# Layer 0's routing with one shared product moved up, and one expert's job in four f32 passes

## The chip, the cores and the metric

The kernel runs on one core of a Trainium2 chip. The metric is device time in microseconds: three runs gave 1667.2, 1667.28 and 1667.38 us, a median of 1667.28 us. The engines are TensorE (PE; PEld is its loading of weights), VectorE (DVE), ScalarE (ACT), GpSimd (POOL) and SyncE (SP), which here issues the loads of weights.

## The reference, cut to what matters

Two layers, each a mixer and then a mixture of experts with one shared expert. In layer 0 the mixture works on 512 tokens: 256 latent ones and 256 of context, four tiles of 128. The part that the change touches:

```python
def moe_ffn(h, w_router, e_bias, w_gate, w_up, w_down, s_gate, s_up, s_down):
    scores = sigmoid(h @ w_router)                     # 64 experts
    _, idx = top_k(scores + e_bias, 8)
    wts = take_along_axis(scores, idx); wts = wts / wts.sum(-1) * 2.5
    # each expert: its tokens, gathered
    a = silu(xb @ w_gate[e]) * (xb @ w_up[e])          # 1024 -> 256, twice
    yb = a @ w_down[e]                                 # 256 -> 1024
    routed = sum over experts of yb * weight
    shared = (silu(h @ s_gate) * (h @ s_up)) @ s_down
    return routed + shared
```

All of it is f32.

## The kernel before

Each layer has a plan, a list of jobs written out in `Plan`. A job is one block of up to 128 tokens. It holds one expert (a single), two of 64 rows (a pair), or parts of experts in lanes of 32 rows. Layer 0 has 42 jobs, numbered 0 to 41. Job 38 is a pair, job 39 is the single of the expert of rank 10, jobs 40 and 41 are pairs.

**The loop of jobs.** TensorE and SyncE run in the order in which the code is written (`manual_schedule`); the order on the other engines comes from the framework's scheduler. For job j the code issues the loads of its weights (`experts`, L1069 and L1074 on SyncE), computes gate and up (`gate_up`, L1337), applies the activation (`act`: ACT L1292, DVE L1293), adds fetched partial sums (`add_fetched`, DVE L1533), transposes job j + 1's tokens (`slots_T`, L1459), scatters pieces of job j - 1's output by a product with a matrix of ones and zeros (`scatter`, PE L1544, summed by DVE L1536), transposes the activation (`act_T`, L1308), computes down (`down`, L1351) and splits the output into two parts for its scatter (`place`, L161). The loads go into a ring of eleven buffers of 1 MB (`w8`). SyncE issues a load as soon as its buffer is free, and so runs ahead of TensorE.

**Four passes or three.** `passes[j]` chooses for a job. With 4 the operands are f32, and each product is one call. With 3 the tokens, the weights and the activation are split into a high and a low part in fp32r (`split`: ACT casts the high part, DVE subtracts it), and each product is three calls: high by high (L165), low by high (L166), high by low (L167). Gate and up are then split in four parts of 128 by 1024 (`gate_up3`), down in two (`down3`). In layer 0 every single after job 2 has 3: jobs 6, 11, 15, 20, 25, 29, 34 and 39.

**The routing of layer 0** stands ahead of the loop, in the code's order. `sh_step(t)` advances the shared expert of tile t by one step: gate; up with the activation's start; transposing the activation (L1308); down with its copies to `acc` (L1351, DVE L1400). `route_step(t)` advances the routing of tile t: transposing `hp`, the normalized tokens (L1053); the router's product with the top 8 (L1130 to L1144). `route_T(t)` transposes the tile's router weights `sg` (L1150). `rank` counts the tokens of each expert (L1170 to L1188) and sorts the experts by count; its result `ordi` names the experts whose weights SyncE loads. `slots` marks which token stands where (DVE L1250 writes `oh`, PE L1258 and L1276 multiply by it, DVE L1280 follows).

Of the kernel before, what the change touches and what calls it, by code (L numbers as in the profile page):

```python
# [118 lines left out]
def tile_block(ctx: ExitStack, tc: tile.TileContext, I, out):  # L119
# [940 lines left out]
    def moe(l, out_of, nt, mp, pre=lambda: None, post=lambda: None):  # L1060
# [16 lines left out]
        def expert_dn(c, e):  # L1077
            d = I["moe_w_down"][l, e]
            if l == 0 or c % 4 != 1:
                return load_dn(d)  # L1080
            wd = [k4([128, D], "dn"), mp.tile([128, D], F32, name="dnx")]
            for j in range(2):
                S.dma_start(wd[j], d.rearrange("o (p j) n -> j p (o n)", j=2)[j])
            return wd
# [63 lines left out]
        def route_T(t):  # L1148
            p = bank()
            T.transpose(p[:NE, :128], sgs.pop(t), ident)  # L1150
            A.copy(wT[:, t], p[:NE, :128])
# [65 lines left out]
        njob = len(jobs)  # L1217
# [190 lines left out]
        def both(xs, j0, xT):  # L1408
            for k in range(2):
                xs[j0 + k] = lambda j, sl, k=k: xT[j // 4][:, j % 4, k * 128 + sl.start:k * 128 + sl.stop]  # L1410
# [33 lines left out]
        def gather(x, idx_col):  # L1444
            G.indirect_dma_start(out=x, out_offset=None, in_=h2d[:n2, :],  # L1445
                                 in_offset=bass.IndirectOffsetOnAxis(ap=idx_col, axis=0),
                                 bounds_check=n2 - 1, oob_is_err=False)

        def slots_T(x, passes):
            if passes == 3:  # L1450
                xT = [k4([128, NJ, 128], "xT", F32R) for _ in range(2)]
            else:
                xT = k4([128, NJ, 128], "xT")
            parts = [lambda j, sl, x=x: x[:, j, sl] for x in (xT if passes == 3 else [xT])]
            yield parts if passes == 3 else parts[0]
            for q in range(2):
                p = bank()
                for j in range(4):
                    T.transpose(p[:, j * 128:j * 128 + 128], x[:, (q * 4 + j) * 128:(q * 4 + j) * 128 + 128], ident)  # L1459
                src = p.rearrange("p (j s) -> p j s", j=4)  # L1460
                if passes == 3:
                    split(xT[0][:, q * 4:q * 4 + 4], xT[1][:, q * 4:q * 4 + 4], src)
                else:
                    A.copy(xT[:, q * 4:q * 4 + 4], src)
                yield

        def gather_mm(j0):

            two = range(j0, min(j0 + 2, njob))
            oh = k2([128, nt, 2, 128], "ohr", F32R)  # L1470
            for t in range(nt):
                for j in two:
                    for c, lane, m, off in jobs[j]:
                        V.tensor_scalar(oh[:, t, j - j0, 32 * lane:32 * (lane + m)], ib[:, off:off + 32 * m],
                                        pos[:, t, c:c + 1], None, op0=OP.is_equal)
            xT = [k4([128, 4, 256], "xT") for _ in range(2)]
            n = len(two) * 128
            yield xT
            for q in range(4):
                p = bank()  # L1480
                for j in range(2):
                    o = p[:, j * 256:j * 256 + n]
                    for t in range(nt):
                        for k in range(2):
                            T.matmul(o, h2p[t][k][:, 2 * q + j], oh[:, t].rearrange("p a b -> p (a b)")[:, :n],  # L1485
                                     start=t == 0 and k == 0, stop=t == nt - 1 and k == 1)
                A.copy(xT[q // 2][:, q % 2 * 2:q % 2 * 2 + 2, :n],
                       p.rearrange("p (j s) -> p j s", j=2)[:, :, :n])
                if q == 1:
                    yield  # L1490
# [184 lines left out]

        passes = []
        for sg_ in jobs:
            passes.append(3 if l == 0 and len(sg_) == 1 and len(passes) > 2 else 4)
        grp, sc = [], iter(())
        over = overflow()  # L1680
        LA = 3 if l == 0 else 2
        with tc.manual_schedule(engines={mybir.EngineType.SP, mybir.EngineType.PE}):
# [11 lines left out]
            def route_step(t):  # L1694
                if t not in routes:
                    routes[t] = route(t, hps.pop(t))
                next(routes[t])
# [22 lines left out]
            def sh_step(*ts):  # L1720
                for t in ts:
                    next(shs[t], None)
# [5 lines left out]
            def slots_until(j):  # L1728
                while ready[0] < min(j, njob):
                    next(more)  # L1730

            xs = {}
            if l == 0:
                sh_step(0, 0)
                route_T(0)
                route_T(1)
                route_step(2)
                sh_step(1, 0)
                route_step(2)
                sh_step(1)  # L1740
                route_step(3)
                sh_step(0)
                route_step(3)
                sh_step(1, 2, 2)
                route_T(2)
                next(rank)
                sh_step(1, 2)
                slots_until(n0)
                affine()
                for j in range(2):  # L1750
                    gather(xgs[j], idx[:, j:j + 1])
                next(rank)
                sh_step(3, 3)
                next(rank)
                sh_step(2)
                tr = slots_T(xgs[0], passes[0])
                xs[0] = next(tr)
                for _ in tr:
                    pass
                next(rank)  # L1760
                sh_step(3)
            else:
                sh_step(0, 0)
                route_step(1)
                sh_step(0)
                route_step(1)
                route_T(0)
                sh_step(0)
                next(rank)
                sh_step(1)  # L1770
                slots_until(n0)
                gm = gather_mm(0)
                affine()
                both(xs, 0, next(gm))
                next(gm)
                next(rank)
                for _ in gm:
                    pass
                next(rank)
                for c in range(NS, NS + 2):  # L1780
                    early[c] = expert_dn(c, ds(S.value_load(ordi[0:1, c:c + 1], min_val=0, max_val=NE - 1), 1))
# [153 lines left out]
    with tc.tile_pool(name="moe0", bufs=1) as mp:  # L1935
        normalize(moe(0, out0, 4, mp, preload_na, mods_na)[0], xt[:2])
# [3 lines left out]
    with tc.tile_pool(name="moe1", bufs=1) as mp:  # L1940
        y = moe(1, out1, 2, mp)[1]
        for t in range(2):
            for n in range(1 + t):
                r = slice(n * 512, n * 512 + D // (1 + t))
                S.dma_start(out[0, t * 128:t * 128 + 128, r], y[t][:, r])
# [85 lines left out]
```

## Time and profile before

| what | value |
|---|---|
| median of three runs | 1667.28 us |
| profiled execution, its own time | 1667.79 us |
| its span | 1666.0 us |
| PE busy | 1560.8 us, 94% |
| DVE busy | 762.9 us, 46% |
| ACT busy | 444.3 us, 27% |
| mean granted TensorE clock | 0.98 of full |
| layer 0's routing | about 240 to 296 us |
| layer 0's jobs | about 296 to 922 us |
| of these job 39 | 862.9 to 887.7 us |

A row of the timeline gives the start, the duration, the engine with line and operation, output and input, and in brackets how long the engine had been idle and what released it. Matmuls are pipelined, so durations overlap and the distance between starts is what one costs; one f32 matmul shows as two records. PEclk is the granted clock of TensorE: 1.00 is 2.4 GHz, 0.50 is 1.2 GHz.

### The profile page before, as it was taken

To read this page: it belongs to the slowest core of one execution; us is meant where nothing else is said; L and a number is where in the kernel's file an instruction comes from. 1 tells how busy PE (TensorE), PEld (TensorE's weight loads), DVE (VectorE), ACT (ScalarE), POOL (GpSimd) and SP (SyncE) were. 2 spreads that over 40 slices of the span, in tenths; PEclk is the share of its full clock that TensorE was granted. 3 is DMA by queue.
4 is the path that set the end of the run, shared out by engine and by line. 5 is a ranking of instruction groups with operands and counts; after the bars stand their busy time and mean duration, and the time that the engine had idled before them with its cause. 6 is when DMAs were issued, how large, how long until landed. Compare 5 with 4: busy or idle time off the path is not lost. (4 is left out here: it accounts for less than half of the span.)

```text
span 1666.0 us, 30733 instructions
## 1 busy us (share of the span) xinstructions
PE 1560.8 (94%) x12138; PEld 1005.9 (60%) x12138; DVE 762.9 (46%) x2077; ACT 444.3 (27%) x882; POOL 174.0 (10%) x162
## 2 busy tenths in 40 slices
PE   7999999999999999999998799999999988989995
PEld 5765687546556566565665577866756654546542
DVE  2475585425455445354566832347443422223225
ACT  2447311113132232232222243332222211112111
POOL 1003210123221121221110000011000000000000
PEclk9999999999999999999999899999999999999998
DMA  9947864799999999989998566247779999999994
GB/s 331 340 172 290 297 233 162 268 366 382 346 398 345 402 401 389 392 327 406 404 407 309 205 212 222 89 181 309 303 316 420 419 419 419 419 420 419 419 420 179
DMA packets 122819, 547.91 MB, mean 329 GB/s; under 512 B 12917, under 2 KB 21509, under 8 KB 74672
## 3 DMA queue, kind: packets, MB, share of 16 engines
q1 hardware_dynamic: 108032, 501.76, 75.6%
q0 software_dynamic: 14640, 44.15, 8.6%
q8 instruction: 97, 1.59, 0.4%
q14 instruction: 50, 0.41, 0.1%
HBM read 532.10 MB, written 21.58 MB: 332 GB/s over the span
## 5 line engine op out<-in xcount | busy, mean ns | idle before, releaser
L1337 PE MATMUL bank<-w,xT 128*32 128x256 f32 (+1 forms) x5696 | 462.8, 388 | 25.8 <-DMA w<-in_moe_w_up_dram 20.2
L1337 PEld LDWEIGHTS bank<-w,xT 128*32 128x32 f32 (+1 forms) x5696 | 276.5, 122 | 204.9 <-DMA w<-in_moe_w_up_dram 28.2
L1351 PE MATMUL bank<-w,aT 128*32 128x512 f32 (+2 forms) x1248 | 235.3, 599 | 3.0 <-ACT aT L1312 2.9
L1293 DVE SCALAR_TENSOR_TENSOR a<-s,wsl,bank 128x256 f32<-128x256 f32 x70 | 33.6, 480 | 407.4 <-ACT s L1292 407.4
L1292 ACT ACTIVATE s<-bank 128x256 f32<-128x256 f32 x70 | 26.9, 385 | 544.5 <-PE bank L1337 496.7
L1544 PE MATMUL bank<-yy,ss 128*128 128x512 f32 x560 | 159.0, 411 | 1.4 <-DVE yy L161 1.1
L1536 DVE TENSOR_TENSOR acc<-acc,bank 128x512 f32<-128x512 f32 x212 | 138.0, 683 | 43.3 <-PE bank L1544 41.6
L1351 PEld LDWEIGHTS bank<-w,aT 128*32 128x32 f32 (+2 forms) x1248 | 68.5, 123 | 120.0 <-issue 104.0
L1544 PEld LDWEIGHTS bank<-yy,ss 128*128 128x128 f32 x560 | 97.3, 191 | 25.9 <-DVE yy L161 5.0
L161 DVE TENSOR_TENSOR yy<-bank,yy 128x512 fp32r<-128x512 f32 x96 | 65.9, 689 | 91.7 <-ACT yy L161 91.7
L161 ACT CAST yy<-bank 128x512 fp32r<-128x512 f32 x96 | 56.2, 586 | 161.6 <-PE bank L1351 144.2
L1445 POOL DMA_INDIRECT xg<-h2d,idx x42 | 52.1, 1239 | 356.8 <-PE bank L1459 181.7
L161 DVE TENSOR_TENSOR wl<-half,wh 128x1024 fp32r<-128x1024 f32 x35 | 42.7, 1224 | 74.4 <-ACT wh L161 74.4
L1250 DVE TENSOR_SCALAR oh<-ib,pos 128x64 bf16<-128x64 bf16 (+3 forms) x432 | 68.7, 245 | 9.7 <-PE bank L1276 9.7
L1516 POOL DMA_INDIRECT accd<-yd,idx x37 | 59.4, 1605 | 128.0 <-issue 92.7
L165 PE MATMUL bank<-wh,hT 128*128 128x512 f32 x160 | 65.2, 407 | 1.7 <-ACT wh L161 1.1
L167 PE MATMUL bank<-wl,hT 128*128 128x512 f32 x160 | 63.4, 396 | 0.5 <-DVE wl L161 0.5
L166 PE MATMUL bank<-wh,hT 128*128 128x512 f32 x160 | 63.2, 395 | 0.3 <-DVE hT L161 0.2
L1485 PE MATMUL bank<-ohr,h2p 128*128 128x256 f32 x448 | 60.8, 289 | 0.0
L1485 PEld LDWEIGHTS bank<-ohr,h2p 128*128 128x128 f32 x448 | 55.3, 191 | 8.2 <-PE bank L1337 4.4
L1437 POOL TENSOR_TENSOR xr<-xr,tmp 128x512 f32<-128x512 f32 x2 | 3.3, 1649 | 478.2 <-DVE tmp L1436 478.2
L1459 PE MATMUL bank<-head,xg 128*128 128x128 f32 x336 | 52.1, 278 | 0.0
(362 smaller groups left out, 2313.2 us busy)
## 6 DMA issues: line engine op xcount, KB each, us to landing
w<-in_moe_w_gate_dram SPq DMA_DIRECT2D x128, 1024.0 KB
w<-in_moe_w_up_dram SPq DMA_DIRECT2D x128, 1024.0 KB
w<-in_moe_w_down_dram SPq DMA_DIRECT2D x104, 1024.0 KB
w<-in_w_mod_dram SPq DMA_DIRECT2D x24, 1024.0 KB
half<-in_na_w_in_dram SPq DMA_DIRECT2D x12, 1024.0 KB
mh<-in_w_mod_dram SPq DMA_DIRECT2D x12, 1024.0 KB
w<-in_w_mod_dram SPq DMA_DIRECT2D x16, 512.0 KB
row<-rowsd POOLq DMA_DIRECT2D x15, 512.0 KB, 8.3
```

Source lines behind the costliest of these rows:

```text
L161: return A.copy(o_h, src), eng.tensor_sub(o_l, src, o_h.bitcast(F32))
L165: T.matmul(p, xh, wh, start=first, stop=False)
L166: T.matmul(p, xl, wh, start=False, stop=False)
L167: T.matmul(p, xh, wl, start=False, stop=last)
L1250: V.tensor_scalar(oh[:, 32 * lane:32 * (lane + m)], ib[:, off:off + 32 * m], pos[:, t, c:c + 1], None, op0=OP.is_equal)
L1337: T.matmul(p[sl, q * FF:q * FF + FF], xT(j, sl), ws[k][0][q][:, j], start=j == 0, stop=j == NJ - 1, **kw)
L1351: T.matmul(p[sl], aT[:, j, sl], d[:, n * 512:n * 512 + 512], start=j == 0, stop=j == 1, **kw)
L1445: G.indirect_dma_start(out=x, out_offset=None, in_=h2d[:n2, :], in_offset=bass.IndirectOffsetOnAxis(ap=idx_col, axis=0), bounds_check=n2 - ...
L1485: T.matmul(o, h2p[t][k][:, 2 * q + j], oh[:, t].rearrange("p a b -> p (a b)")[:, :n], start=t == 0 and k == 0, stop=t == nt - 1 and k == 1)
L1516: G.indirect_dma_start(out=accd[turn_[0]][:, :], out_offset=bass.IndirectOffsetOnAxis(ap=i_, axis=0), in_=y[32 * lane:32 * (lane + m)], in ...
L1536: add = {0: lambda t, r, p: V.tensor_add(acc[t][:, r], acc[t][:, r], p)}
L1544: T.matmul(p, ss[:, t * 128:t * 128 + 128], yy[:, q, r], start=k == 0 and q == 0, stop=k == len(grp) - 1 and q == 1)
```

## The change

Two edits. First, `passes` gives 4 instead of 3 to a single from job 39 on (`njob - 3` is 39), so job 39 alone changes. Second, the first `sh_step` call of layer 0 also takes tile 1's gate product, ahead of `route_T(0)`, and a later call drops its step for tile 1, so that each of tile 1's steps comes one call earlier.

```diff
@@ -1675,7 +1675,7 @@
         passes = []
         for sg_ in jobs:
-            passes.append(3 if l == 0 and len(sg_) == 1 and len(passes) > 2 else 4)
+            passes.append(3 if l == 0 and len(sg_) == 1 and 2 < len(passes) < njob - 3 else 4)
@@ -1731,7 +1731,7 @@
             if l == 0:
-                sh_step(0, 0)
+                sh_step(0, 0, 1)
                 route_T(0)
                 route_T(1)
                 route_step(2)
@@ -1744,7 +1744,7 @@
                 sh_step(1, 2, 2)
                 route_T(2)
                 next(rank)
-                sh_step(1, 2)
+                sh_step(2)
```

On TensorE, from the end of tile 0's shared gate and up to tile 2's shared products, before (w_1828 is the shared gate, w_1830 up, w_1832 down):

```order
L1150 MATMUL bank<-head,sg 64x128 x2
L1053 MATMUL bank<-head,hp 128x128 x8
L1389 MATMUL bank<-w_1828,h2T 128x256 x8
L1308 MATMUL bank<-head,a 128x128 x2
L1130 MATMUL bank<-rw,h2T 128x64 x8
L1389 MATMUL bank<-w_1830,h2T 128x256 x8
L1053 MATMUL bank<-head,hp 128x128 x8
L1351 MATMUL bank<-w_1832,aT 128x512 x4
L1130 MATMUL bank<-rw,h2T 128x64 x8
L1308 MATMUL bank<-head,a 128x128 x2
L1389 MATMUL bank<-w_1828,h2T 128x256 x8
L1389 MATMUL bank<-w_1830,h2T 128x256 x8
```

The same place of TensorE now:

```order
L1389 MATMUL bank<-w_1828,h2T 128x256 x8
L1150 MATMUL bank<-head,sg 64x128 x2
L1053 MATMUL bank<-head,hp 128x128 x8
L1389 MATMUL bank<-w_1830,h2T 128x256 x8
L1308 MATMUL bank<-head,a 128x128 x2
L1130 MATMUL bank<-rw,h2T 128x64 x8
L1308 MATMUL bank<-head,a 128x128 x2
L1053 MATMUL bank<-head,hp 128x128 x8
L1351 MATMUL bank<-w_1832,aT 128x512 x4
L1130 MATMUL bank<-rw,h2T 128x64 x8
L1351 MATMUL bank<-w_1832,aT 128x512 x4
L1389 MATMUL bank<-w_1828,h2T 128x256 x8
```

Tile 1's gate product has moved ahead of the two transpositions of router weights, its up product ahead of tile 0's activation, and its down product (the second L1351) ahead of tile 2's gate; before, that down product stood behind the count of tokens.

On VectorE, at the marks of the first two jobs, in the code's `slots`:

```order
 L1250 TENSOR_SCALAR oh<-ib,pos 128x96
-L1400 COPY acc_2505<-bank 128x512
-L1250 TENSOR_SCALAR oh<-ib,pos 128x32
-L1250 TENSOR_SCALAR oh<-ib,pos 128x64 x6
-L1400 COPY acc_2505<-bank 128x512
-L1250 TENSOR_SCALAR oh<-ib,pos 128x64 x2
+L1250 TENSOR_SCALAR oh<-ib,pos 128x32
+L1250 TENSOR_SCALAR oh<-ib,pos 128x64 x8
 L1250 TENSOR_SCALAR oh<-ib,pos 128x32 x3
 L1280 TENSOR_TENSOR sm<-bank,jm 128x30
```

The two copies of tile 1's shared output no longer stand among the marks; they come earlier, in the routing of tile 3.

On TensorE, job 39 now (w_8772, w_8774 and w_8776 are its gate, up and down):

```order
L1544 MATMUL bank<-yy,ss 128x512 x8
L1337 MATMUL bank<-w_8772,xT 128x256 x8
L1337 MATMUL bank<-w_8774,xT 128x256 x8
L1459 MATMUL bank<-head,xg_1854 128x128 x4
L1544 MATMUL bank<-yy,ss 128x512 x4
L1308 MATMUL bank<-head,a 128x128 x2
L1459 MATMUL bank<-head,xg_1854 128x128 x4
L1544 MATMUL bank<-yy,ss 128x512 x4
L1351 MATMUL bank<-w_8776,aT 128x512 x4
L1544 MATMUL bank<-yy,ss 128x512 x8
```

Before, 48 calls of L165, L166 and L167 stood in place of the sixteen of L1337, and 12 in place of the four of L1351; nothing else of the job differs on TensorE. On VectorE and ScalarE the job's splits of tokens, weights and activation are gone.

## Rows read from the trace of the kernel before

**Rows 1.** The page, its first row.

```profile
span 1666.0 us, 30733 instructions
```

**Rows 2.** Waits of TensorE from 400 to 960 us: total, times, longest.

```profile
PE bank L167 <- DVE wl L161: 9.6, 9, 3.1
```

**Rows 3.** Waits of SyncE's queue from 290 to 960 us, the longest.

```profile
SPq L1074 <- PE bank L1337: 129.1, 26, 17.2
```

**Rows 4.** Timeline of TensorE in jobs 38 and 39, and job 40's start.

```profile
847.23 7.13 PE L1337 MATMUL bank<-w,xT 128*64 128x256 f32 x64
...
862.92 0.28 PE L165 MATMUL bank<-wh,xT 128*128 128x256 f32 x1
...
866.37 0.58 PE L167 MATMUL bank<-wl,xT 128*128 128x256 f32 x1 [3.06 <-DVE wl L161]
...
870.24 0.28 PE L166 MATMUL bank<-wh,xT 128*128 128x256 f32 x1
870.36 0.28 PE L167 MATMUL bank<-wl,xT 128*128 128x256 f32 x1
...
878.31 0.49 PE L166 MATMUL bank<-wh,aTl 128*128 128x512 f32 x1 [1.60 <-DVE aTl L161]
...
880.64 0.80 PE L167 MATMUL bank<-wl,aTh 128*128 128x512 f32 x1 [1.83 <-DVE wl L161]
...
887.72 7.13 PE L1337 MATMUL bank<-w,xT 128*64 128x256 f32 x64
```

**Rows 5.** Windows in job 39: busy PE, PEld, DVE, ACT, POOL; clock, DMA share, GB/s.

```profile
866.30:869.70 3.40, 3.33 (x16) 3.33 (x17) 3.23 (x4) 0.00 (x0) 0.00 (x0) 0.53 1.02 419
...
880.60:886.70 6.10, 6.06 (x15) 4.76 (x16) 2.35 (x3) 1.17 (x2) 0.00 (x0) 0.51 0.60 204
```

**Rows 6.** Timeline of SyncE, job 40's gate and down loads.

```profile
845.28 0.91 SPq L1069 DMA_DIRECT2D w<-in_moe_w_gate_dram  x2
...
854.38 0.90 SPq L1074 DMA_DIRECT2D w<-in_moe_w_down_dram  x2
```

**Rows 7.** Job 38's first addition of fetched sums, the next fetch, and fetches' landing.

```profile
855.30 1.22 DVE L1533 TENSOR_TENSOR acc<-acc,ad 128x1024 f32<-128x1024 f32 x1
...
858.33 1.10 POOL L1525 DMA_DIRECT2D ad<-accd  x2 [0.48 <-issue]
...
DMA to landing us min/median/max: 14.8/14.8/14.8
```

**Rows 8.** Timeline of TensorE in the routing: weight loads, and tile 1's down product.

```profile
241.53 6.78 PEld L1389 LDWEIGHTS bank<-w,h2T 128*128 128x128 f32 x32
...
251.82 0.13 PEld L1150 LDWEIGHTS bank<-head,sg 128*64 128x64 f32 x1 [3.37 <-DVE sg L1143]
...
253.54 4.10 PEld L1389 LDWEIGHTS bank<-w,h2T 128*128 128x128 f32 x16
...
259.78 3.33 PEld L1389 LDWEIGHTS bank<-w,h2T 128*128 128x128 f32 x16
...
269.55 6.79 PEld L1389 LDWEIGHTS bank<-w,h2T 128*128 128x128 f32 x32
...
277.36 3.60 PE L1351 MATMUL bank<-w,aT 128*128 128x512 f32 x8
```

**Rows 9.** Timeline of VectorE: tile 0's activation, and the first marks.

```profile
257.25 0.41 DVE L1302 TENSOR_TENSOR a<-s,bank 128x256 f32<-128x256 f32 x1
...
277.99 1.12 DVE L1250 TENSOR_SCALAR oh<-ib,pos 128x96 bf16<-128x96 bf16 x7
279.28 0.69 DVE L1400 COPY acc<-bank 128x512 f32<-128x512 f32 x1 [0.17 <-PE bank L1351]
...
282.45 0.19 DVE L1280 TENSOR_TENSOR sm<-bank,jm 128x30 f32<-128x30 f32 x1
```

**Rows 10.** Windows at a later group's marks and just behind them.

```profile
312.20:315.70 3.50, 2.47 (x36) 1.78 (x32) 3.36 (x19) 0.00 (x0) 1.54 (x2) 1.00 0.18 75
316.70:320.10 3.40, 3.40 (x20) 1.98 (x18) 1.95 (x15) 0.00 (x0) 2.38 (x3) 0.52 0.84 134
```

## The prediction

> **What bounds the kernel now.** I read the page first, then the waits of TensorE and of SyncE in layer 0's jobs, then the timelines at the two places that the change touches. The span is 1666.0 us [rows 1] and the profiled execution took 1667.79 us, 0.51 us over the median of the runs. In the jobs TensorE never waits for a load: its longest entry there is 9.6 us in 9 waits for VectorE's low parts of weights [rows 2]. SyncE is the one that waits for TensorE, 129.1 us in 26 waits for nothing but a free buffer ahead of the down loads [rows 3]. So in layer 0 the loads run ahead, TensorE's chain sets the time, and each microsecond off it should reach the end, since the layer that follows starts when this one is done.
>
> **Job 39: what goes.** Job 38, a pair in f32, starts its gate and up product at 847.23 and job 39 starts its own at 862.92: a job of the f32 kind takes 15.69 us from start to start [rows 4]. Job 39 lasts from 862.92 to 887.72, 24.80 us [rows 4]. The extra 9.11 us are in the rows: TensorE stands still for 3.06 us before the first low part of gate, 1.60 us before the activation's low part, and 1.83 us before that of down [rows 4], together 6.49 us; and after these stops it works at the lower clock, 0.53 in the 3.40 us behind the first and 0.51 in the 6.10 us behind the last [rows 5], where half of the time is lost, 1.7 and 3.0 us. That is 11.2 us against 9.1 us, since in three passes the products themselves take less.
>
> **Job 39: what comes.** Its sixteen gate and up products and four down products become f32 ones of 128 by 128 weights. The shared expert has the same form: 32 records, sixteen products, issued in 6.78 us [rows 8], and four down products in 3.60 us [rows 8]. The pair's gate and up take 7.13 us [rows 4], so the pair's 15.69 us serve for the new job; by the shared expert's rows it would be up to 0.35 us less. The transpositions and the scatter stay as they are. The casts of ScalarE and subtractions of VectorE go; they were what TensorE waited for, and nothing else waits for them. Job 39's part is 15.69 - 24.80 = -9.1 us, with -9.5 us as its lower end.
>
> In three passes two matmuls start 0.12 us apart [rows 4], so 48 calls are 5.8 us of pure product, while the f32 form takes 6.78 us: more product, less waiting. The Trainium skill, page "FP8 and Floating Point Precision", section "TensorE Precision Notes", says that true f32 takes four passes through the array; read against three passes at the same pace, this speaks against the edit. By that rule the sixteen products would be 64 passes of 0.12 us, 7.7 us, and the job 0.6 us longer than the pair's 7.13 us suggests, so the sum would be 1659.1 us; the 6.78 us of rows 8 say less, and the sum goes by the rows.
>
> **What is late next in job 39.** Two things were covered by the long job. One is job 40's weights, needed 9.1 us sooner, at 862.92 + 15.69 = 878.6. SyncE issued the six loads between 845.28 and 855.3 [rows 6]. From there to 878.6 are 23.3 us, in which the DMA engines move 9.8 MB at 419 GB/s [rows 5], more than nine loads of 1.05 MB; only six loads are asked for, and most of what stood ahead of them is job 39's, in use by then. I cost this at nothing. The other is a fetch of summed outputs. Job 38's first addition starts 855.30 - 847.23 = 8.07 us into the job; in job 39 that would be 871.0. Its fetch is issued at 858.33 and such a fetch lands 14.8 us later, at 873.1 [rows 7]. VectorE may wait 2.1 us. Behind that wait stand the additions that free PSUM banks and, later, job 39's output split, which the next job's scatter reads. VectorE is busy for some 10 of 15.8 us in a pair's job, so it should catch up; I take 0 for TensorE and keep 2.1 us as the upper end.
>
> **Routing: what moves.** TensorE stands still for 3.37 us, until 251.82, for tile 1's router weights [rows 8]. Now tile 1's gate product goes there. Sixteen records take half of 6.78 us, 3.39 us, so it fits almost exactly, and the two transpositions start when they did. At the lower clock that followed the stop, the same product took 4.10 us against 3.33 us for its sister at the full clock [rows 8]; that goes too. But none of this is kept at once: tile 0's activation leaves VectorE at 257.25 + 0.41 = 257.66 [rows 9] whatever TensorE does, because VectorE works through tile 3's norm until then. TensorE, through with the up product at about 256.4, waits 1.3 us. From there to the start of tile 2's shared products, 269.55 [rows 8], TensorE did an up product of 3.33 us and now does a down product of 3.60 us [rows 8] in its place: tile 2's shared products start 0.1 to 0.3 us later than before.
>
> The gain comes behind the count of tokens. There the down product stood, and its two copies of 0.69 us stood among VectorE's marks [rows 9]. The marks now run without them: from 277.99 with seven in 1.12 us [rows 9], nineteen take 3.04 us, and end at 281.0 plus the 0.2 us of delay, against 282.45, where the step behind them starts now [rows 9]. So tile 3's shared products, the sorting of experts and the first load that depends on it come 1.2 us earlier.
>
> The price: from the count (276.6) to the end of the marks (281.2) TensorE now has almost nothing but small matmuls, where it had 3.60 us of down product. The trace shows what follows such a stretch. At a later group's marks, 312.2 to 315.7, TensorE had small work only, and the 3.40 us from 316.7 ran at 0.52 [rows 10]. If tile 3's shared products run at the lower clock for as long, they lose up to 1.7 us; by the sister products above (4.10 against 3.33 us for part of such a stretch) at least 0.8 us. I take 1.5 us. The routing's part is -1.2 + 1.5 = +0.3 us, with -1.2 and +2 as its ends.
>
> **The sum.** -9.1 + 0.3 = -8.8 us: 1659.0 us for the profiled execution's 1667.79 us, and 1658.5 us by the median of the runs. What a measurement of this kernel can tell from no change is about 0.2%, 3.3 us.
>
> **Rivals.**
> 1. The clock stays up behind the marks. For it: TensorE is not idle there, it does some 45 small matmuls and two transpositions. Against it: so it was at 312.2 to 315.7, busy 2.47 of 3.50 us, and the clock fell [rows 10]. Then the routing brings -1.2 us and the time is 1657.0 us. The Trainium skill, page "TensorE: Matmul & The Clock Gate", section "HAM oscillation — how this bites in real kernels", names idle gaps of the engine as what brings the clock down; read so, small matmuls would hold it up and this rival would be the forecast.
> 2. The fetch holds VectorE, and TensorE runs out of PSUM banks or of the output split: 2.1 us at most, 1660.6 us. For it: at job 38 the fetch was already just in time. Against: VectorE's spare time in the job.
> 3. Job 39's gain does not reach the end: a wait later in the layer, or the branch behind it, takes it back. Then only the routing counts, 1667.6 us. Against: the rows show no fixed point between job 40 and layer 1; each load there waits for a buffer that TensorE frees.
> 4. Slower: the loads were the real bound and job 39's stops only hid it. If job 40's weights come no sooner than 887.7, TensorE would stand for 9 us before job 40 and start it at the lower clock, as it did behind the last stop, for 6.10 us [rows 5], losing 3.0 us: 1670.6 us with the routing's 0.3. It decides from the point where those weights land after 887.7, 9.1 us later than they are needed. For it: the DMA share is 1.02 in the middle of job 39. Against: the share falls to 0.60 from 880.6 [rows 5], so the queue had run out, and job 40's loads were ahead of what it then still held.
>
> **How the numbers follow.** The forecast 60%, rival 1 19%, rival 2 12%, rival 3 6%, rival 4 3%. The forecast and rivals 1 and 2 are faster by more than 0.2%: 91%; same 6%; slower 3%. The likeliest case's own range is 1657 to 1660. The range for the time reaches from rival 1 with one stretch of the lower clock fewer in the jobs (1657.0 - 1.7) to rival 2 with one more (1660.6 + 1.7), since every job now begins at another moment: 1655.3 to 1662.3.
>
> **What would show it.** In the changed kernel's profile job 39 should take 15 to 16 us from start to start, with no wait of TensorE for L161 and the clock at 1.00 through job 40's start. The 3.0 us wait for the router weights should be gone, a wait of about 1.3 us for L1302 should stand in its place, and the gathers and first loads behind the marks should come about 1.2 us earlier. Tile 3's shared products should show 0.5 for some 3.4 us. If job 39 stays above 18 us, or a wait for weights stands at job 40, the forecast is wrong at its main term; if the first loads come no earlier, the routing's step is.

## The result, and the profile after

The changed kernel takes 1658.88 us, the median of seven runs (1656.62 to 1663.26), against 1667.28 us before; the ratio is 0.9948, with a 95% interval of 0.9936 to 0.996. By the interval that is 6.7 to 10.7 us faster. The forecast was 1658.5 us.

The profiled execution took 1659.33 us. Its page begins:

```profile
span 1657.2 us, 30680 instructions
```

The span is 8.8 us shorter than before [rows 1]. Where that came from is read from the starts of the jobs' gate and up products on TensorE, in the timelines of both:

| place | before | after | difference so far |
|---|---|---|---|
| tile 2's shared products start | 269.66 | 269.68 | 0.0 |
| job 0 starts | 296.16 | 297.56 | +1.40 |
| job 12 starts | 476.09 | 478.99 | +2.90 |
| job 16 starts | 534.41 | 535.80 | +1.39 |
| job 30 starts | 730.68 | 733.53 | +2.85 |
| job 39 starts | 862.92 | 865.74 | +2.82 |
| job 40 starts | 887.72 | 880.96 | -6.76 |
| layer 1's first product (L279) starts | 927.14 | 918.72 | -8.42 |
| end of the span | 1666.0 | 1657.2 | -8.8 |

TensorE's timeline in jobs 39 and 40, after; it answers to [rows 4]:

```profile
865.74 7.07 PE L1337 MATMUL bank<-w,xT 128*128 128x256 f32 x32
872.64 0.60 PE L1459 MATMUL bank<-head,xg 128*128 128x128 f32 x4
...
875.61 3.60 PE L1351 MATMUL bank<-w,aT 128*128 128x512 f32 x8
...
880.96 7.13 PE L1337 MATMUL bank<-w,xT 128*64 128x256 f32 x64
```

Job 39 lasts from 865.74 to 880.96, 15.22 us instead of 24.80, and the trace shows no wait of TensorE in it. This is the change's gain, -9.58 us.

TensorE's timeline in the routing, after; it answers to [rows 8]. In brackets stands how long the engine had waited:

```profile
252.72 0.38 PE L1150 MATMUL bank<-head,sg 128*64 128x128 f32 x2
...
257.80 0.51 PE L1308 MATMUL bank<-head,a 128*128 128x128 f32 x2 [0.36 <-DVE a L1302]
...
278.23 0.48 PE L1308 MATMUL bank<-head,a 128*128 128x128 f32 x2 [0.70 <-DVE a L1302]
...
281.07 10.01 PE L1389 MATMUL bank<-w,h2T 128*128 128x256 f32 x32
291.02 0.27 PE L1200 MATMUL bank<-perm,pid 64*1 64x64 f32 x2
```

The wait for tile 1's router weights is gone. Tile 3's shared products (the 10.01 us) start 1.45 us earlier than before, but took 7.17 us then. TensorE's timeline of before, at these products and the two that follow them:

```profile
282.52 7.17 PE L1389 MATMUL bank<-w,h2T 128*128 128x256 f32 x32
289.62 0.27 PE L1200 MATMUL bank<-perm,pid 64*1 64x64 f32 x2
```

Why they take longer now, the windows show (columns as in [rows 5]):

```profile
276.60:280.00 3.40, 2.38 (x29) 1.75 (x27) 2.87 (x18) 1.16 (x4) 0.00 (x0) 1.00 0.00 0
280.00:283.40 3.40, 3.22 (x14) 2.45 (x15) 2.41 (x19) 0.00 (x0) 1.07 (x1) 0.50 0.01 2
283.40:286.80 3.40, 3.40 (x10) 2.68 (x9) 0.00 (x0) 0.00 (x0) 1.03 (x1) 0.50 0.64 183
...
865.70:881.00 15.30, 15.30 (x69) 11.49 (x68) 8.28 (x13) 3.10 (x6) 0.00 (x0) 1.00 1.01 413
...
474.60:478.00 3.40, 3.40 (x10) 2.63 (x9) 0.90 (x1) 0.32 (x1) 0.12 (x1) 0.50 1.00 419
...
720.30:723.70 3.40, 3.40 (x18) 3.40 (x18) 2.10 (x2) 0.29 (x1) 0.00 (x0) 0.51 1.01 426
```

From 276.6 to 280.0 TensorE has the marks' small matmuls and is busy 2.38 of 3.40 us at the full clock; then it runs at 0.50, 1.2 GHz, until 286.8, twice as long as behind the later marks of [rows 10]. Job 39 runs at 1.00 throughout. The last two windows, in jobs 11 and 29, are stretches at the lower clock that the trace of before does not have. It has two others, in job 15 and in job 41's down product, which the trace of the changed kernel does not have:

```profile
521.30:524.70 3.40, 3.40 (x19) 3.40 (x18) 2.18 (x3) 0.00 (x0) 0.00 (x0) 0.51 1.01 424
...
917.30:920.70 3.40, 3.40 (x10) 0.98 (x8) 0.67 (x2) 0.59 (x1) 0.00 (x0) 0.50 0.02 8
```

These explain the table's other steps: +1.5 at job 11, -1.5 at job 15, +1.5 at job 29, -1.7 at job 41. The last -0.4 us, in layer 1, were not followed further.

VectorE's timeline after, at the first marks and in job 39; it answers to [rows 9] and [rows 7]:

```profile
278.00 2.84 DVE L1250 TENSOR_SCALAR oh<-ib,pos 128x96 bf16<-128x96 bf16 x19
280.94 0.19 DVE L1280 TENSOR_TENSOR sm<-bank,jm 128x30 f32<-128x30 f32 x1
...
876.87 1.22 DVE L1533 TENSOR_TENSOR acc<-acc,ad 128x1024 f32<-128x1024 f32 x1 [1.33 <-DMA ad<-accd]
```

The step behind the marks (L1280) starts 1.5 us earlier, at 280.94 against 282.45, and VectorE waits 1.33 us for a fetch in job 39. SyncE's first load behind the routing, after:

```profile
292.87 0.36 SPq L1069 DMA_DIRECT2D w<-in_moe_w_gate_dram  x1
```

The same load before:

```profile
291.48 0.36 SPq L1069 DMA_DIRECT2D w<-in_moe_w_gate_dram  x1
```

It is issued 1.4 us later, not earlier.

### The profile page after: what moved, and what is told of

Its sections match the earlier page's. It is cut to its first block, busy times and chain, and to the rows that moved or that the text cites. A ratio compares the mean times of both kernels' runs of the same rounds, so it can differ in the third digit from the quotient of the medians.

```text
span 1657.2 us, 30680 instructions
## 1 busy us (share of the span) xinstructions
PE 1560.2 (94%) x12118; PEld 1005.5 (61%) x12118; DVE 754.0 (45%) x2068; ACT 438.7 (26%) x876; POOL 173.6 (10%) x162
## 5 line engine op out<-in xcount | busy, mean ns | idle before, releaser
L1337 PE MATMUL bank<-w,xT 128*32 128x256 f32 (+2 forms) x5728 | 470.3, 388 | 25.2 <-DMA w<-in_moe_w_up_dram 19.7
L1337 PEld LDWEIGHTS bank<-w,xT 128*32 128x32 f32 (+2 forms) x5728 | 284.1, 123 | 204.0 <-issue 28.4
L1351 PE MATMUL bank<-w,aT 128*32 128x512 f32 (+2 forms) x1256 | 237.2, 596 | 3.0 <-ACT aT L1312 2.9
L1351 PEld LDWEIGHTS bank<-w,aT 128*32 128x32 f32 (+2 forms) x1256 | 69.6, 123 | 120.3 <-issue 103.4
L165 PE MATMUL bank<-wh,hT 128*128 128x512 f32 x160 | 65.2, 407 | 1.7 <-ACT wh L161 1.1
L167 PE MATMUL bank<-wl,hT 128*128 128x512 f32 x160 | 63.2, 395 | 0.5 <-DVE wl L161 0.5
L166 PE MATMUL bank<-wh,hT 128*128 128x512 f32 x160 | 63.2, 395 | 0.3 <-DVE hT L161 0.2
```

The lines of the kernel that those rows point to most:

```text
L165: T.matmul(p, xh, wh, start=first, stop=False)
L166: T.matmul(p, xl, wh, start=False, stop=False)
L167: T.matmul(p, xh, wl, start=False, stop=last)
L1337: T.matmul(p[sl, q * FF:q * FF + FF], xT(j, sl), ws[k][0][q][:, j], start=j == 0, stop=j == NJ - 1, **kw)
L1351: T.matmul(p[sl], aT[:, j, sl], d[:, n * 512:n * 512 + 512], start=j == 0, stop=j == 1, **kw)
```

## The experiments

Besides the change nine kernels ran, each with the kernel before on the same chip beside it. A ratio of 0.001 is 1.7 us.

| kernel | median, us | lowest to highest | ratio to before, 95% interval |
|---|---|---|---|
| the change | 1658.88 | 1656.62 to 1663.26 | 0.9948 (0.9936 to 0.996) |
| e1_job39_only | 1658.08 | 1655.13 to 1658.72 | 0.9944 (0.9927 to 0.996) |
| e2_routing_only | 1667.82 | 1666.7 to 1669.94 | 1.0009 (1.0 to 1.0019) |
| e3_down_behind_count | 1653.72 | 1651.97 to 1654.71 | 0.9921 (0.9905 to 0.9937) |
| e4_fill_marks | 1656.61 | 1655.03 to 1660.4 | 0.9944 (0.9927 to 0.9961) |
| e5_job34_four | 1659.64 | 1657.6 to 1660.42 | 0.9951 (0.9936 to 0.9967) |
| e6_fill_later_marks | 1651.18 | 1650.28 to 1652.4 | 0.9903 (0.9886 to 0.9921) |
| e7_stopping_singles_four | 1646.57 | 1643.14 to 1649.15 | 0.9883 (0.9864 to 0.9901) |
| e8_no_fetched_sums | 1659.47 | 1657.07 to 1661.79 | 0.9943 (0.9926 to 0.9959) |
| e9_all_stopping_four | 1646.97 | 1645.12 to 1647.84 | 0.9874 (0.9858 to 0.9891) |

**Each half alone.** e1 takes back the routing's edit, e2 that of job 39; their diffs against the changed kernel:

```diff
# e1_job39_only
-                sh_step(0, 0, 1)
+                sh_step(0, 0)
...
-                sh_step(2)
+                sh_step(1, 2)
# e2_routing_only
-            passes.append(3 if l == 0 and len(sg_) == 1 and 2 < len(passes) < njob - 3 else 4)
+            passes.append(3 if l == 0 and len(sg_) == 1 and len(passes) > 2 else 4)
```

> The edit of job 39 alone; the routing's order is that of the kernel before. Theory (in the changed kernel the routing costs 1.4 us, since tile 3's shared products start 1.45 us earlier but take 10.0 instead of 7.2 us): job 0 starts at 296.2 us as before, job 39 takes 15.2 us, and the time is 1658.9 - 1.4 = 1657.5 us. Rival (the routing gains its 1.2 us by itself, and what is missing went elsewhere): 1660.1 us. Stretches at the lower clock in the jobs, of about 1.5 us each, may stand elsewhere than in either kernel.

> The edit of the routing alone; job 39 stays in three passes. Theory: job 0 starts at 297.6 us instead of 296.2, job 39 still takes about 24.8 us with its stops for low parts, and the time is 1667.3 + 1.4 = 1668.7 us. Rival (the routing's order gains 1.2 us): 1666.1 us. A second rival (job 39's stops depend on when its weights land, and the routing's shift changes them): job 39 more than 1.5 us off 24.8.

Job 39's edit alone is worth all of the gain (0.9944), and the job took 15.23 us. The routing's alone is no gain: 1.0009, nothing to 3 us slower. By that interval the theory's 1667.3 + 1.4 is possible, the rival's 1666.1 us is not. That e1 is faster than the whole change is not shown by its time, since the intervals overlap. In e2's profiled execution job 39 took 23.84 us, within the bound set.

Both expectations missed where job 0 starts: at 298.73 in e1 instead of 296.2, and at 295.18 in e2 instead of 297.6. TensorE's timeline of e1, a window of e1 at the same place, and tile 1's gate product (the x16) as before had it:

```profile
255.26 5.35 PE L1389 MATMUL bank<-w,h2T 128*128 128x256 f32 x16
...
298.73 7.12 PE L1337 MATMUL bank<-w,xT 128*32 128x256 f32 x128
```

```profile
255.30:258.70 3.40, 3.40 (x10) 2.68 (x10) 3.40 (x4) 0.59 (x1) 0.53 (x1) 0.50 1.02 428
```

```profile
253.75 4.29 PE L1389 MATMUL bank<-w,h2T 128*128 128x256 f32 x16
```

The order of before has its own stretch at the lower clock, behind the wait for tile 1's router weights, and in e1 it lasted 6.8 us instead of 3.4. So the +1.40 us at job 0 in the first table is the difference of two executions and not yet the price of the new order. From the start of tile 0's shared products to job 0 the old order took 54.57, 56.31 and 55.10 us (before, e1, and e8 below), the new one 55.25, 53.51 and 54.95 us (the change, e2, and e5 below). These ranges overlap: the traces show neither a loss nor a gain of the whole routing. The part behind the start of tile 2's shared products is steadier: 26.50, 26.49 and 26.50 us against 27.88, 26.62 and 27.72 us.

Tile 3's shared products took less long in e2 than in the changed kernel; TensorE's timeline of e2:

```profile
279.85 8.86 PE L1389 MATMUL bank<-w,h2T 128*128 128x256 f32 x32
...
295.18 7.11 PE L1337 MATMUL bank<-w,xT 128*32 128x256 f32 x128
```

At the full clock the same products took 7.17 us, so the price of the lower clock was 1.7 us in that execution and 2.8 us in the other.

**Is it the clock?** e4 fills the marks of the changed kernel with work for nobody:

```diff
                 next(rank)
+                busy(3)
                 sh_step(2)
+                busy(5)
```

> The changed kernel with eight products of 128 by 128 of a constant, whose result nobody reads: three behind the count, five behind the transposition of tile 2's activation, where TensorE mostly waits. Theory (the lower clock of tile 3's shared products follows from TensorE's idle time between the count and the end of the marks): the clock stays at 1.00, these products take 7.2 instead of 10.0 us, from a start at 281.1 to 281.5 us; job 0 starts at 294.7 to 295.1 us, and the time is 1656.0 to 1656.5 us. Rival (small products do not hold the clock, or it falls for another reason): 10.0 us as in the changed kernel, and 1658.9 to 1659.3 us.

TensorE's timeline of e4, and its windows from the count on:

```profile
279.85 7.17 PE L1389 MATMUL bank<-w,h2T 128*128 128x256 f32 x32
```

```profile
275.70:279.10 3.40, 3.40 (x45) 3.06 (x41) 3.09 (x20) 1.12 (x4) 0.00 (x0) 1.00 0.00 0
279.10:282.50 3.40, 3.30 (x21) 2.82 (x20) 2.23 (x18) 0.00 (x0) 1.25 (x2) 1.00 0.01 2
```

The clock stayed at 1.00 and the same products took 7.17 us. From the start of tile 2's shared products (268.56) to job 0 (293.49) were 24.93 us; the changed kernel needed 27.88, the kernel before 26.50. So behind that point the routing's edit gains 1.6 us without the lower clock; with it, it loses 1.4 us in the changed kernel's trace and 0.1 and 1.2 us in those of e2 and e5. The time alone (1656.61 us, but 0.9944 with a wide interval) would not have settled that. That the fill is what held the clock rests on this one trace, against three without fill.

**A better order.** e3 leaves tile 1's gate product where the change puts it, and moves its down product back behind the count:

```diff
-                sh_step(1, 2, 2)
+                sh_step(2, 2)
                 route_T(2)
                 next(rank)
-                sh_step(2)
+                sh_step(1, 2)
```

> Both edits, but tile 1's shared down product stands behind the count of tokens, where it stood before. Theory (the count waits for nothing but TensorE's own order: VectorE has tile 3's choice of experts at 267.7 us, the count starts at 276.7): without the 3.5 us of the down product ahead of it the count starts at 273.1 us; the down product fills TensorE behind it, so that tile 3's shared products start at 279.0 us at the full clock and take 7.2 us; job 0 starts at about 292.7 us instead of 297.6, and the time is 1658.9 - 4.9 = 1654.0 us. Rival (the first experts' weights or something else than TensorE sets job 0's start): job 0 at 296 to 297 us, 1657 to 1658 us. Second rival (the lower clock comes behind the marks in any case): tile 3's products 10 us, job 0 at 295.5 us, 1656.9 us.

TensorE's timeline of e3:

```profile
264.71 7.13 PE L1389 MATMUL bank<-w,h2T 128*128 128x256 f32 x32
...
272.46 3.60 PE L1351 MATMUL bank<-w,aT 128*128 128x512 f32 x8
...
277.62 7.17 PE L1389 MATMUL bank<-w,h2T 128*128 128x256 f32 x32
...
291.26 7.11 PE L1337 MATMUL bank<-w,xT 128*32 128x256 f32 x128
```

Tile 2's shared products start 4.97 us earlier than in the changed kernel; 1.48 of that is that this execution was earlier from the start (tile 0's activation, L1302, started on VectorE at 255.85 instead of 257.33), 3.5 us the down product. It now fills the stretch behind the count, and the clock holds. Job 0 starts 6.30 us earlier, 4.82 us without the 1.48; expected were 4.9. The median is 1653.72 us. The rivals fall: in this trace neither weights nor a lower clock behind the marks hold job 0.

**Where do four passes pay?** e5 gives them to job 34, which hardly stops; e7 takes e3 and gives them to jobs 11, 15 and 29, which do; e9 adds job 6:

```diff
# the change, and e3
-            passes.append(3 if l == 0 and len(sg_) == 1 and 2 < len(passes) < njob - 3 else 4)
# e5_job34_four, against the change
+            passes.append(3 if l == 0 and len(sg_) == 1 and 2 < len(passes) < njob - 8 else 4)
# e7_stopping_singles_four, against e3
+            passes.append(3 if l == 0 and len(sg_) == 1 and len(passes) in (6, 20, 25, 34) else 4)
# e9_all_stopping_four, against e3
+            passes.append(3 if l == 0 and len(sg_) == 1 and len(passes) in (20, 25, 34) else 4)
```

> The changed kernel with job 34, too, in four f32 passes. In three it takes 13.22 us and its stops for low parts are only 1.0 us. Theory (four passes cost about 1.8 us more product, and pay only where a job loses more than that to stops and to the lower clock behind them): job 34 takes 15.2 us like job 39, and the time is 1658.9 + 2.0 = 1660.9 us. Rival (f32 is the better form for a single in any place): job 34 at 13.2 us or less, 1658.9 us or less.

> The kernel of e3_down_behind_count with jobs 11, 15 and 29 in four f32 passes as well; jobs 6, 20, 25 and 34 stay in three. In e3 these three take 15.53, 15.74 and 15.71 us; in the changed kernel they stop for parts for 2.0, 2.7 and 3.4 us. Theory (four passes pay where a job stops): each takes what the f32 pairs beside it take less 0.4 us, so 13.4, 13.6 and 13.3 us; together -6.7 us, 1647 us; by product alone (1.8 us more each, stops of 8.1 us gone, two stretches at the lower clock of 1.5 us gone) -5.7 us, 1648 us. Rival (the stops only wait for what is late anyway, and four passes cost their 1.8 us): 1653.7 + 5.4 = 1659 us.

> The kernel of e7_stopping_singles_four with job 6 in four passes too; jobs 20, 25 and 34 stay in three. In three, job 6 takes 13.94 us and stops 1.8 us for parts. Theory (four passes pay where the stops are longer than the added product, which was 1.3 us in e5_job34_four: 13.49 us with 1.0 us of stops gone, against 13.22): job 6 at 13.4 us, 1646.6 - 0.5 = 1646 us, less than can be told by time alone. Rival (job 11's gain in e7 was mostly the lower clock): job 6 at 13.9 to 14.7 us, 1646.6 to 1647.4 us.

TensorE's timeline of e5, job 34 and the start of job 35:

```profile
788.27 7.17 PE L1337 MATMUL bank<-w,xT 128*128 128x256 f32 x32
...
798.24 3.60 PE L1351 MATMUL bank<-w,aT 128*128 128x512 f32 x8
801.76 0.44 PE L1337 MATMUL bank<-w,xT 128*64 128x256 f32 x2
```

Job 34 takes 13.49 us instead of 13.22: the direction of the theory, but 0.3 us and not 2.0. I had taken job 39's whole length for it, which holds eight scatter products more than job 34, some 2 us (between its down products at 875.61 to about 879 and job 40's start at 880.96). By time e5 (1659.64 us) can't be told from the change. In e7 jobs 11, 15 and 29 took 13.30, 13.98 and 13.48 us against 15.53, 15.74 and 15.71 in e3, and the wait of 1.7 us that stood ahead of job 29 went too. The waits of TensorE from 440 to 860 us, first e3, then e7 (total, times, longest):

```profile
PE bank L167 <- DVE wl L161: 4.7, 7, 1.8
PE bank L166 <- DVE aTl L161: 3.6, 6, 0.8
...
PE bank L165 <- ACT wh L161: 1.7, 1, 1.7
```

```profile
...
PE bank L167 <- DVE wl L161: 2.1, 4, 0.7
PE bank L166 <- DVE aTl L161: 1.7, 3, 0.6
```

e7's 1646.57 us is 7.2 us under e3; expected were 5.7 to 6.7. Its profiled execution, 1643.14 us, was the fastest of its four, and two other jobs differed in it as well: job 1 kept the full clock (12.89 instead of 14.58 us), and job 25, still in three passes, took 14.54 instead of 13.39 us, with 0.8 us more of stops. In e9 job 6 took 13.52 instead of 13.94 us, near the 13.4 expected, and the time can't tell it from e7. e7 and e9 are the fastest kernels here, some 20 us under the kernel before.

**Why did job 39 stop so long, and job 34 not?** In the kernel before, VectorE adds the fetched sums in jobs 36 to 39, and job 39 is the only three-pass job there. e8 leaves out those of tiles 2 and 3, four of the eight, which stand in jobs 38 and 39; its output lacks these sums:

```diff
-                    for k in range(2):
+                    for k in range(2 if t < 2 else 0):
                         V.tensor_add(acc[t], acc[t], y[:, k])
```

> The kernel before, job 39 in three passes, with the additions of fetched sums for tiles 2 and 3 left out (they stand on VectorE in jobs 38 and 39, 2.4 us in each, so the output lacks them). Theory (job 39 stops because its low parts queue on VectorE behind these additions and what they push back; it is not the three passes as such): job 39 takes 14 to 17 us instead of 24.8, and the time is 1657.5 to 1661 us. Rival (the low parts come late because of ScalarE's casts or the weights' landing): job 39 stays above 20 us and the time above 1662 us.

TensorE's timeline of e8, what is left of the stops in job 39, and job 40's start:

```profile
868.76 0.39 PE L167 MATMUL bank<-wl,xT 128*128 128x256 f32 x1 [1.25 <-DVE wl L161]
876.84 0.50 PE L166 MATMUL bank<-wh,aTl 128*128 128x512 f32 x1 [0.55 <-DVE aTl L161]
879.17 0.50 PE L167 MATMUL bank<-wl,aTh 128*128 128x512 f32 x1 [0.44 <-DVE wl L161]
882.11 7.13 PE L1337 MATMUL bank<-w,xT 128*64 128x256 f32 x64
```

Stops of 2.24 us instead of 6.49, no lower clock behind them, and the job took 16.44 us in three passes (it started at 865.67). The theory holds: without these additions the job is 8.4 us shorter in three passes, so most of its cost was VectorE's queue, not three passes as such. Four passes are still 1.2 us better in that place, with the additions in.

**Fill in other places.** e6 takes e3 and fills the marks of the next two groups:

```diff
                 c0 = min(sg_[0] for sg_ in jobs[j])
+                if l == 0 and j0 in (2, 6):
+                    busy(2 if j0 == 2 else 1)
                 if j in sent and len(jobs[j]) > 1:
```

> The kernel of e3_down_behind_count with products of a constant, whose result nobody reads, in the marks of the next two groups: two for each of jobs 2 to 5, one for each of jobs 6 to 13. In e3 job 1 starts behind the first of these at the lower clock and takes 14.58 us, against 12.89 us in e1_job39_only, where the clock stayed up there; job 4's gate and up take 8.55 us against 7.11 us at the full clock. Theory (TensorE's idle time in the marks brings the clock down): both stretches at 1.00, job 1 at 12.9 us and job 4 1.4 us shorter, 1653.7 - 3.1 = 1650.6 us, up to 0.5 us more where the added products delay the marks' own. Rival (fill does not hold the clock, or the lower clock comes a little later instead): 1653.7 to 1654.7 us.

Windows of e6, at the first of these groups and at the second:

```profile
310.80:314.20 3.40, 3.40 (x40) 2.59 (x41) 3.27 (x28) 0.00 (x0) 2.54 (x2) 1.00 0.42 41
...
352.40:355.80 3.40, 3.18 (x38) 2.38 (x34) 3.16 (x17) 0.00 (x0) 1.42 (x2) 1.00 1.01 422
355.80:359.20 3.40, 3.00 (x29) 1.67 (x32) 3.09 (x27) 0.00 (x0) 1.37 (x2) 0.51 1.02 410
```

At the first group the clock held (job 1's gate and up 7.13 us, in e3 8.81); but it held there in e1 and e7 as well, without fill, so this does not show that the fill did it. At the second group the theory failed: with one added product per job the clock fell, for longer than in e3, and job 4 took 15.99 us instead of 14.70. The 2.5 us that its median is under e3 are not explained by the fill: in the profile the 1.4 us of job 1 are more than given back at jobs 2 to 4 (+0.6, +0.4, +1.3), and what is faster are jobs 11 (-1.6), 28 and 29 (-2.9), with job 15 slower (+1.5), none of which the fill touches. What it is worth stays open.

## Why the prediction was right, point by point

**Job 39, right; its size just past the lower end.** Forecast -9.1, with -9.5 as its end; measured -9.58. The term that was a little off is "the pair's 15.69 us serve for the new job". Gate and up took 6.90 us up to the next product (865.74 to 872.64), the pair's 7.05 (847.23 to 854.28); the rest of the job, up to the next job's start, took 8.32 us, the pair's 8.64. The shared expert's rows, the other bound, were nearer. The Trainium skill's four passes ("FP8 and Floating Point Precision", "TensorE Precision Notes"), priced at the pace of rows 4, gave an estimate of 7.7 us for this product; the trace says 6.90. That four passes cost more than three where TensorE stops little (1.0 us in job 34), e5 shows, by 0.3 us.

**What is late next, right.** Job 40 waited for no weights: job 39 ran with the DMA share at 1.01, and from 290 to 960 us SyncE still waits 126.8 us in 27 waits for the buffers that L1337 frees, much as before [rows 3]. The fetch held VectorE for 1.33 us, within the 2.1, and TensorE not at all. Rivals 2 and 4 are out.

**Routing: the mechanism right, the price too small in this trace, and one claim wrong.** The gain was sized at -1.2 us and measured at -1.45 (tile 3's start); the price at +1.5 and measured at +2.84, so in this pair of traces the part is +1.4 instead of +0.3 us. The step that was mis-sized is "if tile 3's shared products run at the lower clock for as long" as the 3.40 us of [rows 10]: they ran at it for 6.8 us. The windows and e4's 7.17 us show the clock to be the whole price: without the fill it fell there in each of the three traces with this order (the change, e2 and e5), with it, in the one trace there is, it did not. In e2 the price was 1.7 us, close to the forecast, so the length differs between executions. The wait for L1302 was 0.36 us and not 1.3: in this execution TensorE came 0.7 us later into the routing (241.59 before, 242.31 after), with VectorE where it was. That none of the gain ahead of this wait is kept does not hold for every trace of the old order: in e1 the longer lower clock there put tile 2's shared products 13.49 us behind the start of tile 0's activation on VectorE (L1302), against 12.41 in before and 12.35 in the changed kernel.

The claim that "the first load that depends on it" comes 1.2 us earlier was wrong. The experts' sorting ends in two products on TensorE (L1200, L1201), and these stand behind tile 3's shared products. They moved from 289.62 to 291.02, and the load with them, by +1.4 us. I had followed VectorE's marks and not the queue of TensorE behind them. In e4, where tile 3's shared products kept the full clock, the load came sooner: 20.25 us behind the start of tile 2's shared products, against 21.82 before and 23.19 in the changed kernel. The claim's failure cost nothing more, as job 0 was late by the same 1.4 us and did not wait.

**Rival 1, wrong, and with it the rule's reading.** The small matmuls did not hold the clock. The Trainium skill, page "TensorE: Matmul & The Clock Gate", section "HAM oscillation — how this bites in real kernels", speaks of idle gaps. Here the longest wait that the trace names between the count and tile 3's products is 0.70 us, and the clock fell all the same.

**Rival 3, wrong.** Job 40's gain of 6.76 us reached the end whole; 1.7 us came on top because job 41's down product kept the full clock.

**Stretches at the lower clock.** The range allowed one more or one fewer in the jobs. There were two new and two fewer, -0.2 us together. The prediction's reason, that every job begins at another moment, does not sort them: in seven traces (the change, e1 to e5 and e8), whose job 11 starts between 457.0 and 463.5 us, they stood in jobs 11 and 29, and in before and e6, whose job 11 starts at 462.1 and 459.7 us, one stood in job 15 instead. What puts them there is open. That the seven runs of the changed kernel spread over 6.6 us is probably the same thing; no run here shows it, since each kernel has one trace.

**The sum, right in part by luck.** The span's -8.8 us is the forecast's figure to the tenth, but the terms are not: job 39 came out 0.5 us better, the routing 1.1 us worse, and the clock elsewhere and layer 1 gave the 0.6 us back. What more than one pair of traces shows is the new job 39: 15.21 to 15.23 us in seven more kernels (e1, e3 to e7, e9). The old one took 24.80 us in before and 23.84 in e2.

## What to carry to other kernels

A split into fewer, cheaper passes pays only where the engine that makes the parts has them ready: price each place by its own stops and by the clock behind them, since the same form cost 13.2 us in job 34 and 24.8 us in job 39. Moving work out of a stretch to close a wait opens that stretch; look at what TensorE has left there, and if it is small matmuls only, reckon with the lower clock behind it, 1.7 to 2.8 us here (e3 kept the gain by leaving the down product there). And read a difference of a microsecond or two from several traces of each order: here one pair said +1.4 us where three of each overlap. And where a count or a sort is late, ask what stands ahead of it on the engine's own queue before looking for what it waits for.

## What was not expected of the hardware

The lower clock lasted 6.8 us behind the marks in the changed kernel, and 3.4 us behind others. And a stretch that the records show as busy for 3.18 of 3.40 us, at 1.00 and mostly in small matmuls, was followed by the lower clock (e6, 352.4 to 355.8), while e7's first later marks, where TensorE was busy 2.37 of 3.40 us, were not. Windows of e7:

```profile
307.40:310.80 3.40, 2.37 (x33) 1.66 (x32) 3.35 (x19) 0.00 (x0) 1.59 (x2) 1.00 0.13 53
310.80:314.20 3.40, 3.40 (x35) 2.32 (x34) 2.80 (x23) 0.00 (x0) 2.52 (x3) 1.00 0.83 121
```

e9 differs from e7 in job 6 alone, far behind these marks. Its windows there:

```profile
306.80:310.20 3.40, 2.37 (x33) 1.66 (x33) 3.25 (x19) 0.00 (x0) 1.69 (x2) 1.00 0.11 46
310.20:313.60 3.40, 3.40 (x18) 1.95 (x20) 2.79 (x23) 0.00 (x0) 2.52 (x3) 0.54 0.86 124
```

In both, TensorE has the same matmuls in the marks, with the same two named waits of 0.36 and 0.21 us, and job 1 then took 12.89 us in e7 and 14.58 in e9. So neither the busy share nor the order of the small matmuls tells, in these rows, whether the clock holds; what does was not found here.
